# Later planned times for turned queries and keys, score banks and output transpositions in a hybrid attention step

## The chip, the cores and the metric

The kernel runs on one core of a Trainium2 chip. The metric is device time in microseconds (us). A core has five engines that each work through a queue of their own in the order in which the program issued it: TensorE (PE in the profile: matrix products), VectorE (DVE), ScalarE (ACT), GpSimd (POOL) and SyncE (SP), which here issues every DMA. They wait for each other through semaphores.

## The reference

The reference is one layer of a decoder step with 2048 prompt positions and 32 sample positions (8 sequences of 4). Two attention branches read the same normalised input; their outputs are gated, merged and projected:

```python
def prompt_layer(x, ...):
    qa, ka, va, ga, qb, kb, vb, gb, ma, mb = mixer_inputs(x, ...)   # rmsnorm, x @ w_in, QK-norm
    o_a, _ = banded_window_attention(qa, ka, va, 1, 128, rel_bias[:, :8], sink)
    for gi, (win, dil) in enumerate(((128, 1), (512, 4), (2048, 16))):
        o, lse = banded_window_attention(qb[:, :, gi, :, None, :], kb[:, :, gi], vb[:, :, gi],
                                         dil, win // dil, rel_bias[:, c0:c0 + 8], None)
    o_b = combine_dilations(outs, lses)        # weights proportional to softmax denominators
    y = mixer_output(x, o_a, o_b, ga, gb, ma, mb, w_up_a, w_up_b, w_out)

def mixer_output(x, o_a, o_b, ga, gb, ma, mb, w_up_a, w_up_b, w_out):
    ya = (o_a * silu(ga)) @ w_up_a
    yb = (o_b * silu(gb)) @ w_up_b
    return x + (sigmoid(ma) * ya + sigmoid(mb) * yb) @ w_out
```

Each query sees a window of 128 keys of its residue class, with a bias by distance. Branch A has 8 query heads of 64 on 2 key heads, branch B three groups of 8 heads. The 32 sample positions do the same against cached keys and values. Window rows of keys and values are outputs too.

## The kernel before, in words

**A planner writes the order.** The kernel is emitted by Python that carries a clock of its own. `Clock` (`ck`) has the planned time `ck.now`, a planned time at which ScalarE, VectorE and GpSimd become free (`use` adds a duration and gives the planned end) and a planned DMA queue (`move` sets `ck.come`, the planned landing of the transfer just issued). Generators are processes: what they yield is the planned time at which they go on. `ck.now` advances with every matmul that is issued (`mm`) and where the main thread waits for a condition. None of this exists on the chip. It decides only in which order instructions are put on each queue; the waits on the chip follow from the data. If the planner believes a result to be there earlier than it is, the instruction that reads it stands at the head of its queue and holds up what is behind it.

**Splits.** Products keep accuracy with two float16 parts of each operand, hi and lo (`split`, lines 303 to 308), and three matmuls for each product.

**Stages.** First the input is normalised and turned into `hT`, and the merge gates are computed (0 to some 400 us). Then come branch B's groups 3, 2 and 1, and branch A (to some 1840 us), each over 16 tiles of 128 positions. Last are the up-projections and the output projection. In the attention the main thread (`tile_order`, `steps`) issues projections tile by tile: query, key and value (in A also two gates), each 24 matmuls into a PSUM bank, on line 259 with the operands `slot` (weights) and `hT`. The work behind each is a chain that runs beside the main thread:

- `q_chain`: raw copy (L730), norm (L738 to L751), split by `parts`, then `turn` (line 764): one DMA transposition, SP's line 167, after which the chain waits until `ck.come`; then `qn`, the scratch of normed queries, is given back and `t.q` is set.
- `k_chain`: the same for keys, after `prev.scored` (all scores of the tile before issued); `k_turn` (line 769) calls `turn` and then issues two copies on VectorE (L773) that exchange the two halves of the partitions. Then `kn` is given back and `t.k` is set.
- `attend` starts when `t.q` and `t.k` are set and the tile before is scored. It spawns 2 units where a tile sees one key block, else 4.
- `unit`: takes one of two score banks (`S_l`), issues the score matmuls (L259, operands `arena`, shapes 128x128 or 128x256), then on VectorE the bias add with row maximum (L801), which empties the bank. `S_l[y].put()` gives it back in the plan. Then exponentials on ScalarE (L815), the split, a DMA transposition of the probabilities, a margin of 1800 ns, and the matmuls with the values (L259, shape 128x64) into bank 7.
- `to_pairs`, in branch A's `finish2` and once for the samples: VectorE scales the gated outputs (L1340), then, after a margin of 200 ns, eight transpositions on TensorE (L263) and splits into `hT`.

Beside all this run the sample positions' attention (GpSimd and VectorE, with reads of the caches) and the conversion of weights (L470, L473). At a change of group the bias tables are loaded anew, when the last tile has used them.

## Time and profile before

| | us |
|---|---|
| median of 3 runs (2163.1 to 2168.06) | 2163.2 |
| profiled execution | 2170.46 |
| its span, first to last instruction | 2168.6 |

The profile shows one execution. Busy time and idle time are in us; a wait is named by the line that waited and the line that ended its wait. "L259" is the helper that issues nearly all matmuls, so its groups are told apart by the names of tiles and by shapes: `bank<-slot,hT` are projections, `bank<-arena` is attention. `arena` is one large scratch tile that holds nearly all that moves between the engines.

### The profile page before, as it was taken

Reading aid. Unit: us, or ns where it says so; the run is one execution under the profiler, and the core shown is the slowest. Engines: PE = TensorE matmul, PEld = TensorE weight load, DVE = VectorE, ACT = ScalarE, POOL = GpSimd, SP = SyncE. Lnnn points to the kernel's source line nnn. Section 1 sums busy time; section 2 is a strip of 40 time slices with the busy share of each in tenths; the row PEclk is TensorE's granted clock in tenths of the full one; section 3 lists DMA queues with packets and bytes.
Section 4 is the critical chain, followed back from the end, with each engine's and each line's share of the span. In section 5 each row is a group of like instructions: output and inputs, shape, how many; then the busy total and the mean of one; then the engine's idle time right before and its main releaser. Section 6 shows DMA issues by size and latency. Waiting matters only on the chain.

```text
span 2168.6 us, 36145 instructions
## 1 busy us (share of the span) xinstructions
PE 2029.2 (94%) x13042; PEld 1135.8 (52%) x13042; DVE 1386.0 (64%) x3305; ACT 1053.3 (49%) x2526; POOL 707.9 (33%) x530
## 2 busy tenths in 40 slices
PE   6999999999999899898999999997899997999999
PEld 3555555666665455554544554544455555444464
DVE  5546662576754577773767885869788898642331
ACT  5432312555555667665776766765456555300000
POOL 1000000255632245541324552426655653220110
PEclk9999999999999999999999999999999998999999
DMA  7896571368879568978857878744434366332322
GB/s 225 175 300 230 203 269 57 115 175 201 217 174 264 139 134 203 215 157 228 218 113 151 168 167 160 172 102 107 79 82 108 96 176 175 110 107 88 115 85 93
DMA packets 528389, 344.34 MB, mean 159 GB/s; under 512 B 397585, under 2 KB 427762, under 8 KB 528210
## 3 DMA queue, kind: packets, MB, share of 16 engines
q1 hardware_dynamic: 528210, 342.04, 61.4%
q8 instruction: 102, 1.67, 0.3%
q14 instruction: 77, 0.63, 0.1%
HBM read 193.53 MB, written 62.43 MB: 118 GB/s over the span
## 4 chain that ended last, share of the span: by engine, by line
PE 59%; DVE 15%; DMA 12%; ACT 5%; issue 4%; SPq 2%; POOL 2%; DVEq 0%; POOLq 0%; ACTq 0%
PE bank L259 58%; DMA arena<-arena 7%; DVE arena L308 3%; DVE arena L773 2%; DMA out_dram<-arena 2%; DVE slot L473 2%; DVE arena L801 2%; ACT arena L815 2%; SPq L161 1%; SPq L167 1%; ACT slot L470 1%; DMA hT<-arena 1%; ACT arena L303 1%; DVE arena L751 1%; POOL nst L743 1%
## 5 line engine op out<-in xcount | busy, mean ns | idle before, releaser
L259 PE MATMUL bank<-slot,hT 128*128 128x512 f16 (+1 forms) x4992 | 1127.6, 377 | 8.0 <-ACT arena L730 4.5
L259 PEld LDWEIGHTS <-hT 128*128 128x128 f16 x4992 | 546.8, 113 | 436.5 <-issue 45.2
L259 PE MATMUL bank<-hT,slot 128*128 128x416 f16 (+4 forms) x2928 | 530.8, 342 | 17.7 <-DVE slot L473 3.8
L743 POOL TENSOR_TENSOR nst<-nst,nhalf 128x8 f32<-128x8 f32 (+2 forms) x136 | 232.4, 1710 | 773.9 <-DVE nst L741 704.6
L259 PEld LDWEIGHTS <-slot 128*128 128x128 f16 x2928 | 287.2, 99 | 251.1 <-DVE slot L473 11.1
L259 PEld LDWEIGHTS <-arena 128*128 128x128 f16 x4336 | 267.9, 99 | 283.1 <-issue 88.9
L259 PE MATMUL bank<-arena 128*128 128x64 f16 (+5 forms) x3746 | 269.9, 230 | 88.6 <-DVE arena L773 44.5
L815 ACT ACTIVATE arena<-arena,ast,inv 128x256 f32<-128x256 f32 (+1 forms) x512 | 283.8, 555 | 7.0
L308 DVE SCALAR_TENSOR_TENSOR arena<-arena 128x512 f16<-128x512 f32 (+1 forms) x292 | 221.6, 772 | 92.2 <-ACT arena L303 91.2
L303 ACT ACTIVATE arena<-arena 128x512 f16<-128x512 f32 (+2 forms) x395 | 231.3, 607 | 98.6 <-DMA arena<-arena 53.8
L1172 POOL TENSOR_TENSOR arena<-arena 128x512 f32<-128x512 f32 (+1 forms) x102 | 140.1, 1373 | 120.7 <-DVE arena L1215 101.4
L259 PE MATMUL bank<-slot,arena 128*128 128x512 f16 x768 | 167.9, 379 | 2.1 <-DVE slot L473 1.6
L473 DVE SCALAR_TENSOR_TENSOR slot<-slot,gsc 128x512 f16<-128x512 f32 (+1 forms) x144 | 107.3, 745 | 86.7 <-ACT slot L470 86.2
L730 ACT ACTIVATE arena<-bank 128x512 f32<-128x512 f32 x112 | 65.8, 589 | 173.4 <-PE bank L259 89.4
L643 ACT ACTIVATE arena<-bank,wst 128x416 f32<-128x416 f32 (+2 forms) x82 | 48.7, 597 | 190.5 <-PE bank L259 162.9
L470 ACT ACTIVATE slot<-slot,gsc 128x512 f16<-128x512 f32 (+1 forms) x144 | 98.1, 681 | 73.2 <-DVE slot L473 63.7
L303 ACT ACTIVATE arena<-arena,yk 128x512 f16<-128x512 f32 (+2 forms) x40 | 25.5, 638 | 201.1 <-POOL arena L1706 186.4
L1706 POOL TENSOR_TENSOR arena<-arena 128x512 f32<-128x512 f32 (+2 forms) x40 | 48.7, 1218 | 221.2 <-DVE arena L1692 201.7
L801 DVE CUSTOM_DVE_ANT_0 arena<-bank,bias 128x128 f32<-128x128 f32 (+1 forms) x296 | 87.4, 343 | 50.2 <-PE bank L259 48.9
L740 DVE TENSOR_REDUCE nst<-arena 128x8 f32<-128x512 f32 (+2 forms) x136 | 85.6, 630 | 42.3 <-ACT arena L738 41.6
L773 DVE COPY arena<-arena 64x1024 f16<-64x1024 f16 (+1 forms) x128 | 77.5, 605 | 54.0 <-DMA arena<-arena 52.3
L810 ACT ACTIVATE ast<-ast,ninv 128x2 f32<-128x2 f32 (+1 forms) x212 | 61.2, 289 | 102.6 <-DVE ast L801 101.7
(167 smaller groups left out, 1758.5 us busy)
## 6 DMA issues: line engine op xcount, KB each, us to landing
arena<-in_cache_b_kv_dram SPq DMA_DIRECT2D x144, 256.0 KB
slot<-in_w_in_dram SPq DMA_DIRECT2D x64, 512.0 KB
arena<-Qs SPq DMA_DIRECT2D x96, 256.0 KB
arena<-in_w_in_dram SPq DMA_DIRECT2D x16, 1024.0 KB
gates<-arena SPq DMA_DIRECT2D x78, 208.0 KB
comb<-arena SPq DMA_DIRECT2D x48, 264.0 KB
arena<-comb SPq DMA_DIRECT2D x48, 264.0 KB
arena<-gates SPq DMA_DIRECT2D x24, 512.0 KB
```

What stands on the lines that cost most here:

```text
L259: T.matmul(out, l, r, start=start, stop=stop)
L303: A.activation(hi, src, AF.Copy, scale=scale)
L308: V.scalar_tensor_tensor(lo, src, scale, hi, op0=OP.mult, op1=OP.subtract)
L470: A.activation(b.part(0, k), src, AF.Copy, scale=sc)
L473: V.scalar_tensor_tensor(b.part(1, k), src, sc, b.part(0, k), op0=OP.mult, op1=OP.subtract)
L730: A.activation(dst, src, AF.Copy)
L740: V.tensor_reduce(st[:, 0, :nh], heads(s), axis=AX.X, op=OP.add)
L743: G.tensor_tensor(st[:, 2, :nh], st[:, 1, :nh], nhalf[p0:p0 + n].to_broadcast([n, nh]), op=OP.pow)
L773: V.tensor_copy(y[64 - 64 * j:128 - 64 * j], x[64 * j:64 * j + 64])
L801: V.tensor_tensor_reduce(out=o, in0=i_, in1=b_, scale=1.0, scalar=-3e38 if g else sinkS[:, u, j:j + 1], op0=OP.add, op1=OP.max, accum_out= ...
L815: A.activation(e, e, AF.Exp, bias=nm[:, x:x + 1], scale=inv[:, g:g + 1], accum_out=l[:, x:x + 1])
L1172: G.tensor_tensor(sprod[:n], q, k, op=OP.mult)
```

## The change

Three planned times change. After a turned block the chain goes on 1500 ns later; a score bank counts as free 500 ns after the point at which it did; the margin ahead of the output transpositions is 900 ns for 200. No instruction is added, removed or altered.

```diff
     def turn(dst, src, nh):
 
         SP.turn(dst, src[:, :nh * 64].bitcast(F16))
-        yield ck.come
+        yield ck.come + 1500
...
         while t.biased in t.used:
             t.biased += 1
         yield e
-        S_l[y].put()
+        ck.at(ck.now + 500, S_l[y].put)
         A.activation(nm[:, xs_], m[:, xs_], AF.Copy, scale=ninv[:, g:g + 1])
...
         yield use("V", tv(512) + 500)
-        yield ck.now + 200
+        yield ck.now + 900
         for i in range(2):
             b = yield from tbank()
```

## The prediction

> **What bounds the kernel now.** I read the page first: the busy shares, the chain that ended last, then the span and mean granted clock of the core.

> ```profile
> span 2168.6 us, 36145 instructions
> PE 2029.2 (94%) x13042; PEld 1135.8 (52%) x13042; DVE 1386.0 (64%) x3305; ACT 1053.3 (49%) x2526; POOL 707.9 (33%) x530
> PE 59%; DVE 15%; DMA 12%; ACT 5%; issue 4%; SPq 2%; POOL 2%; DVEq 0%; POOLq 0%; ACTq 0%
> core 0: 2168.6 us, clock 0.979
> ```

> TensorE (PE) is busy for 2029.2 of 2168.6 us. So 139 us are idle, and that is nearly all that a change of order can win. The chain agrees: 59% PE, most of the rest links that PE stood waiting for. Next I read the waits of PE and of VectorE (DVE): who waited, for what, us in total, how often, the longest.

> ```profile
> PE bank L259 <- DVE arena L773: 44.5, 32, 4.7
> PE bank L259 <- DMA arena<-arena: 27.8, 20, 6.5
> PE bank L259 <- DVE ast L801: 12.6, 7, 4.0
> PE bank L263 <- DVE arena L1340: 7.4, 6, 2.4
> DVE arena L773 <- DMA arena<-arena: 52.3, 34, 4.6
> ```

> The largest wait is for L773, the copies that swap the halves of a turned key block; DVE in its turn stands 52.3 us waiting for the turning DMA ahead of them. L801 is the bias add that empties a score bank; L1340 scales the pairs that to_pairs transposes. These three belong to the three edits. The DMA row is mixed, so I took PE's groups with shapes kept apart:

> ```profile
> L259 PE MATMUL bank<-arena 128*128 128x64 f16 x2544 | 112.5, 196 | 24.1 <-DMA arena<-arena 23.7 <-DVE arena L1459 0.2
> L259 PE MATMUL bank<-arena 128*128 128x256 f16 x672 | 106.8, 277 | 36.4 <-DVE arena L773 22.2 <-DVE ast L801 12.6 <-DMA arena<-arena 1.0
> L259 PE MATMUL bank<-arena 128*128 128x128 f16 x352 | 30.2, 226 | 25.6 <-DVE arena L773 22.3 <-DMA arena<-arena 3.2
> ```

> Shapes 128x128 and 128x256 are scores, 128x64 is probabilities times values. So 4.2 us (1.0 + 3.2) of the DMA waits are scores waiting for the turned block itself, and 23.7 us are value products waiting for turned probabilities, whose margin (1800 ns in unit) the change leaves alone. Now one ordinary tile in the timeline, 18.3 us from the first of its score rows to that of the next tile (start, duration, instruction, count, idle before it and its releaser):

> ```profile
> 554.67 0.55 PE L259 MATMUL bank<-arena 128*128 128x128 f16 x7 [0.94 <-DVE arena L773]
> 559.34 0.61 PE L259 MATMUL bank<-arena 128*128 128x128 f16 x8
> 559.79 9.88 PE L259 MATMUL bank<-slot,hT 128*128 128x512 f16 x45
> 570.81 2.13 DVE L773 COPY arena<-arena 64x1024 f16<-64x1024 f16 x2 [1.70 <-DMA arena<-arena]
> 571.84 0.22 PE L259 MATMUL bank<-arena 128*128 128x128 f16 x1
> 572.99 0.55 PE L259 MATMUL bank<-arena 128*128 128x128 f16 x7 [0.94 <-DVE arena L773]
> 574.68 0.51 PE L259 MATMUL bank<-arena 128*128 128x64 f16 x12
> ```

> DVE had nothing to do for 1.70 us, then copied from 570.81 to 572.94. PE had reached the scores at 571.84, ran the one matmul that needs no copy, and stood 0.94 us. Projection matmuls for the coming tile were there (45 of them in 9.88 us, 0.22 us each), but they stand behind the scores in PE's queue. The kernel's planner believed the turn and the copies to be done earlier than they were.

> **The change part by part.** No instruction is added or removed, and no new wait on the chip; only the planner's clock moves, and with it the order on each queue. Line 773 has 128 copies, two for each of 64 tiles, so turn is delayed 128 times in the plan, once for queries and once for keys of each tile.

> *Turned queries and keys, +1500 ns.* Nearly seven projection matmuls (1.5/0.22) now go ahead of each tile's scores. On DVE the copies fall behind what is ready in 1.5 us; where DVE idled, as at 570.81, they run at the same moment as before. The transposing DMA itself does not move; the probabilities' DMAs, bias reloads and stores behind the scores move on SP's queue with their tile. A wait of up to 1.5 us goes, a longer one loses 1.5. Ten of the 32 L773 waits are longer:

> ```profile
> 496.69 0.55 PE L259 MATMUL bank<-arena 128*128 128x128 f16 x7 [1.64 <-DVE arena L773]
> 516.54 0.72 PE L259 MATMUL bank<-arena 128*128 128x128 f16 x7 [1.79 <-DVE arena L773]
> 689.47 0.91 PE L259 MATMUL bank<-arena 128*128 128x128 f16 x7 [4.72 <-DVE arena L773]
> 740.83 0.55 PE L259 MATMUL bank<-arena 128*128 128x128 f16 x7 [3.36 <-DVE arena L773]
> 811.75 0.49 PE L259 MATMUL bank<-arena 128*128 128x256 f16 x3 [1.95 <-DVE arena L773]
> 911.09 0.91 PE L259 MATMUL bank<-arena 128*128 128x128 f16 x7 [3.79 <-DVE arena L773]
> 1113.23 0.49 PE L259 MATMUL bank<-arena 128*128 128x256 f16 x3 [1.99 <-DVE arena L773]
> 1469.62 1.44 PE L259 MATMUL bank<-arena 128*128 128x256 f16 x15 [2.71 <-DVE arena L773]
> 1502.15 1.39 PE L259 MATMUL bank<-arena 128*128 128x256 f16 x11 [4.15 <-DVE arena L773]
> 1568.59 1.44 PE L259 MATMUL bank<-arena 128*128 128x256 f16 x15 [3.04 <-DVE arena L773]
> ```

> They sum to 29.1; the other 22 to 15.4. Saved: 10 x 1.5 + 15.4 = 30.4 us. The 4.2 us for the turned block fall under the same margin, but some stand right before a copy wait of the same scores and would be counted twice:

> ```profile
> 473.45 0.22 PE L259 MATMUL bank<-arena 128*128 128x128 f16 x1 [0.97 <-DMA arena<-arena]
> 475.00 0.55 PE L259 MATMUL bank<-arena 128*128 128x128 f16 x7 [1.33 <-DVE arena L773]
> ```

> Here 0.97 + 1.33 is cut by 1.5, not by 2.3. I take 2.2 off for all such pairs: **30.4 + 4.2 - 2.2 = 32.4 us**. Cover gone (no projections left to put ahead), the saving there is 0.

> *Score banks free 500 ns later.* The shortest of the 7 L801 waits exceeds 0.5:

> ```profile
> 1082.46 0.60 PE L259 MATMUL bank<-arena 128*128 128x256 f16 x4 [0.57 <-DVE ast L801]
> ```

> So **7 x 0.5 = 3.5 us**, with projections as cover again.

> *Output transpositions 700 ns later* (900 for 200; 17 passes through to_pairs). Two of the six L1340 waits are shorter than that:

> ```profile
> 1587.30 0.63 PE L263 MATMUL bank<-ident,arena 128*128 128x128 f32 x4 [0.25 <-DVE arena L1340]
> 1745.37 0.63 PE L263 MATMUL bank<-ident,arena 128*128 128x128 f32 x4 [0.32 <-DVE arena L1340]
> ```

> The others save 0.7 at most: **4 x 0.7 + 0.57 = 3.4 us**.

> *The clock.* Stretches around long waits (length, busy times, granted clock, DMA share):

> ```profile
> 516.00:521.00 5.00, 4.46 (x29) 2.67 (x29) 4.14 (x16) 2.41 (x4) 1.23 (x1) 0.66 0.54 184
> 686.00:696.00 10.00, 6.53 (x31) 3.72 (x31) 6.86 (x25) 5.53 (x15) 5.06 (x3) 0.66 0.88 261
> 908.00:918.00 10.00, 6.91 (x37) 3.42 (x37) 6.22 (x16) 5.03 (x16) 6.60 (x5) 0.66 0.78 180
> 1502.00:1508.00 6.00, 5.85 (x38) 3.63 (x38) 5.76 (x18) 2.67 (x7) 3.32 (x4) 0.72 0.05 14
> ```

> Each costs (1 - clock) x length: 1.7, 3.4, 3.4, 1.7, together 10.2 us, of which I take **6**, since waits of 2.3 to 3.2 us remain at the last three (bounds 0 and 10.2). [...]

> *What is given back.* First, at the changes of stage, when few projections are ready, a later chain is a later end. Four stretches, 680:760, 960:1010, 1460:1575 and 1789:1843, have together (sum row of the windows):

> ```profile
> sum 299.00, PE 242.19 PEld 142.62 DVE 213.77 ACT 162.85 POOL 124.47; mean PE 60.55 PEld 35.65 DVE 53.44 ACT 40.71 POOL 31.12
> ```

> 57 us of PE idle, the densest in the attention. I charge one turn and one bank margin for each: 4 x (1.5 + 0.5) = **8 us** (bounds 0 and 50, below). Second, the value product at 574.68 belongs to the scores at 559.34, and the wait at 572.99 lies between them. Take it away, and PE reaches the product 0.94 us earlier against the same chain of DVE, ScalarE and DMA. The 23.7 us of waits for turned probabilities can grow; I take **5 us** (bounds 0 and 12: 13 such waits of the 20 DMA waits, 0.94 each).

> Sum: 32.4 + 3.5 + 3.4 + 6 - 8 - 5 = 32.3 us off the span of 2168.6, that is 2136.3. The profiled execution took 2170.5 us as a whole, so 2138; against the median of the runs, 2163.2, it is **2131**.

> **The rivals.** *Everything behind the copies comes loose.* DVE stands 52.3 us in front of them with ready work behind, so ScalarE and the probability chains also run ahead, and the waits go whole: 44.5 + 4.2 - 2.2 + 12.6 + 7.4 + 10.2 = 77 us, nothing given back: 2086. For it: the idle row of L773. Against: the longest waits exceed the margins by up to 3 us. Between this and the forecast lies about 2105.

> *The waits only change their name.* In the ordinary stretch the DMA engines are nearly full:

> ```profile
> 552.00:592.00 40.00, 37.19 (x242) 25.47 (x241) 29.43 (x71) 23.03 (x61) 25.66 (x18) 1.00 0.85 221
> ```

> If transfers at 0.85 set the pace, a faster PE finds turned probabilities that much later, the 23.7 us grow by what was won, and the time is 2160 to 2166. Against: the stretch still has 15% free, and the tile would need only 5% more (0.94 of 18.3 us).

> *Slower: the chain of tiles at a change of stage decides.* Key turns wait for the tile before to be scored. If the last three and first two tiles run one after another there, each pays the turn and two bank margins, 1.5 + 2 x 0.5 = 2.5 us: 5 x 2.5 = 12.5 for a change, 50 for four. The gains inside these stretches go too: the waits at 689, 740, 1469, 1502 and 1568 (5 x 1.5), a few tenths beside, and the 6 us of clock. Left elsewhere: 32.4 - 8.3 + 3.5 + 3.4 - 5 = 26. Net 24 slower: 2187. It decides against the change from (26 + 6.5)/4 = 8 us for each change. Against it: in the ordinary tile the last scores end at 559.95 and the copies of the next start at 570.81, so 10.9 us lie between, against a turn of a few us; PE's work, not that chain, sets the period of 18.3.

> **How the numbers follow.** A measurement of this kernel can tell 0.3%, 6.5 us, from no change. The forecast (2112 to 2148) has 0.55, the larger gain 0.13 (2080 to 2112), a gain of 2148 to 2156 0.07, changed names 0.13 (within 0.3%), slower 0.12. So faster 0.75, same 0.13, slower 0.12. The range 2100 to 2168 leaves out the slower case and the far end of the larger gain; cost bounds of 50 and 12 against 45 of gains reach past its upper end only in the slower case.

> **What would show it.** The L773 row of PE's waits falls from 44.5 to about 14, DVE's wait in front of the copies from 52.3 by a third or more; L801 to about 9; L1340 to about 4; scores waiting for a turned block to near 0; 128x64 products waiting for DMA rise to about 29; the mean granted clock rises from 0.979 to about 0.982. Wrong: if the L773 row falls and PE's idle total stays at 139, the names only changed; if idle time in the four stretches exceeds 57 + 32, the slower case holds; if waits of several us remain at ordinary tiles, the order shifted elsewhere.

## The result: 1.4% slower

The changed kernel takes 2195.24 us (median of 4 runs, 2192.91 to 2196.6), the kernel before 2163.41 in the same rounds. The ratio is **1.0141** (95% interval 1.0123 to 1.0158). The forecast was 2131, with slower at a chance of 0.12 and the range ending at 2168. Here is the changed kernel's page and its core row:

```profile
span 2194.0 us, 36053 instructions
PE 2027.6 (92%) x13042; PEld 1134.7 (52%) x13042; DVE 1388.6 (63%) x3305; ACT 1051.9 (48%) x2526; POOL 713.1 (33%) x530
core 0: 2194.0 us, clock 0.974
```

The busy time of every engine is that of before to within 1%. The span grew by 25.4 us, and all of it is TensorE standing idle. Its waits, and VectorE's in front of the key copies:

```profile
PE bank L259 <- DVE arena L773: 37.9, 23, 5.0
PE bank L259 <- DMA arena<-arena: 36.8, 23, 5.1
PE bank L259 <- ACT arena L999: 15.4, 4, 6.0
PE bank L259 <- ACT arena L730: 10.5, 8, 6.6
PE bank L263 <- DVE arena L1340: 7.1, 4, 2.8
PE bank L259 <- DVE ast L801: 3.6, 2, 2.7
DVE arena L773 <- DMA arena<-arena: 25.2, 15, 4.4
```

VectorE's idle time in front of the copies halved (52.3 to 25.2), and the waits behind a score bank fell from 12.6 to 3.6. But the wait for the copies fell only from 44.5 to 37.9 where about 14 was forecast, and two rows grew: projections that wait for L999 and L730. These are ScalarE's raw copies out of a PSUM bank, L999 of a value block, L730 of a query or key block, and a projection waits for them when no bank is free. In the kernel before the two rows had 6.7 us together, now they have 25.9. ScalarE's own waits tell why. First TensorE's two rows and ScalarE's two in the kernel before:

```profile
PE bank L259 <- ACT arena L730: 4.5, 1, 4.5
PE bank L259 <- ACT arena L999: 2.2, 1, 2.2
ACT arena L730 <- DMA out_dram<-arena: 80.1, 13, 10.6
ACT arena L999 <- DMA out_dram<-arena: 24.0, 7, 10.3
```

then ScalarE's in the changed one:

```profile
ACT arena L730 <- DMA out_dram<-arena: 93.2, 14, 9.5
ACT arena L999 <- DMA out_dram<-arena: 56.4, 15, 9.7
```

The raw copies write into staging rows, `stK` for keys and `stV` for values, one each, from which window rows are stored to memory. The next copy into a row must wait until the store of the tile before has landed. The planner gives a row back (`stK_l.put()`, `stV_l.put()`) where it issues the store, not where the store lands. So the copy gets to the head of ScalarE's queue too early and holds up all that is behind it. In group 3 every one of the 16 tiles stores both rows, in group 2 four, in group 1 one.

Where in time was it lost? Each group has one sample projection (L891) at its third tile, so from one of them to the next is one group's work. The first two in the kernel before (start, duration):

```profile
420.12 2.12 PE L891 MATMUL bank<-slot,hT 128*32 128x512 f16 x27
766.73 5.36 PE L891 MATMUL bank<-slot,hT 128*32 128x512 f16 x72
```

and in the changed one:

```profile
418.26 0.83 PE L891 MATMUL bank<-slot,hT 128*32 128x512 f16 x9
788.33 5.36 PE L891 MATMUL bank<-slot,hT 128*32 128x512 f16 x72
```

Group 3 took 370.1 us for 346.6. Worked out in the same way, groups 2 and 1 together took 686.8 for 684.0, and from there to the first output projection 434.0 for 433.0. **23.5 of the 25.4 us were lost in group 3.** Counted in projection matmuls, 72 to a tile, its first eight tiles took 4.8 us less than before. Tiles 9 to 14 took 139.8 us for 116.2, with TensorE's waits in them 24.2 for 5.0. From there to the third tile of group 2, with the end of the group and the change to the next, it was 94.7 for 91.2. So the loss came ahead of the change of group. The timeline of an ordinary tile there, in the changed kernel (start, duration, instruction, idle before it and its releaser):

```profile
564.82 0.47 SPq L161 DMA_DIRECT2D out_dram<-arena  x1
568.12 0.69 ACT L999 ACTIVATE arena<-bank,wst 128x512 f32<-128x512 f32 x1 [4.23 <-DMA out_dram<-arena]
569.37 0.69 DVE L308 SCALAR_TENSOR_TENSOR arena<-arena 128x512 f16<-128x512 f32 x1 [3.01 <-ACT arena L303]
578.83 0.22 PE L259 MATMUL bank<-arena 128*128 128x128 f16 x1 [0.82 <-DMA arena<-arena]
579.14 0.42 SPq L161 DMA_DIRECT2D out_dram<-arena  x1
581.30 0.55 PE L259 MATMUL bank<-arena 128*128 128x128 f16 x7 [2.25 <-DVE arena L773]
583.37 0.60 ACT L730 ACTIVATE arena<-bank 128x512 f32<-128x512 f32 x1 [5.58 <-DMA out_dram<-arena]
```

The value rows' store goes out at 564.82; the next value copy has stood on ScalarE for 4.23 us until it ran at 568.12. The softmax parts (L303) and the split on VectorE behind it (L308) come late by it. The key row's store goes out at 579.14, and the next key copy costs ScalarE 5.58 us more. TensorE has issued 60 projection matmuls since the last scores, where the tile of before that the prediction shows had 45, and still finds the turned block (0.82) and the copies (2.25) missing. In that tile of before it lost 0.94.

### The profile page after: what moved, and what is told of

The parts are those of the page before. It is cut to its first block, busy times and chain, and to the rows that moved or that the text cites. A ratio compares the mean times of both kernels' runs of the same rounds, so it can differ in the third digit from the quotient of the medians.

```text
span 2194.0 us, 36053 instructions
## 1 busy us (share of the span) xinstructions
PE 2027.6 (92%) x13042; PEld 1134.7 (52%) x13042; DVE 1388.6 (63%) x3305; ACT 1051.9 (48%) x2526; POOL 713.1 (33%) x530
## 4 chain that ended last, share of the span: by engine, by line
PE 52%; DVE 15%; DMA 12%; ACT 7%; issue 6%; POOL 5%; SPq 3%; ACTq 0%; POOLq 0%; DVEq 0%
PE bank L259 50%; DMA arena<-arena 4%; DMA out_dram<-arena 4%; DVE arena L308 3%; ACT arena L815 2%; DVE arena L801 2%; ACT arena L303 2%; POOL nst L743 2%; SPq L167 2%; SPq L161 1%; DVE slot L473 1%; POOL arena L1172 1%; DVE arena L773 1%; DVE arena L751 1%; DMA hT<-arena 1%
## 5 line engine op out<-in xcount | busy, mean ns | idle before, releaser
L259 PE MATMUL bank<-slot,hT 128*128 128x512 f16 (+1 forms) x4992 | 1128.8, 377 | 30.3 <-ACT arena L999 15.4
L259 PEld LDWEIGHTS <-hT 128*128 128x128 f16 x4992 | 547.6, 113 | 468.1 <-issue 74.9
L259 PE MATMUL bank<-hT,slot 128*128 128x416 f16 (+4 forms) x2928 | 529.0, 341 | 26.7 <-DVE slot L473 10.7
L743 POOL TENSOR_TENSOR nst<-nst,nhalf 128x8 f32<-128x8 f32 (+2 forms) x136 | 232.4, 1709 | 762.9 <-DVE nst L741 694.8
L259 PEld LDWEIGHTS <-slot 128*128 128x128 f16 x2928 | 287.0, 99 | 259.1 <-issue 16.1
L259 PEld LDWEIGHTS <-arena 128*128 128x128 f16 x4336 | 266.7, 100 | 268.1 <-issue 64.4
L259 PE MATMUL bank<-arena 128*128 128x64 f16 (+5 forms) x3746 | 265.6, 233 | 80.0 <-DVE arena L773 37.9
L308 DVE SCALAR_TENSOR_TENSOR arena<-arena 128x512 f16<-128x512 f32 (+1 forms) x292 | 227.6, 791 | 158.1 <-ACT arena L303 149.0
L303 ACT ACTIVATE arena<-arena 128x512 f16<-128x512 f32 (+2 forms) x395 | 232.4, 607 | 85.0 <-DVE arena L751 36.1
L259 PE MATMUL bank<-slot,arena 128*128 128x512 f16 x768 | 167.9, 379 | 2.2 <-DVE slot L473 1.6
L730 ACT ACTIVATE arena<-bank 128x512 f32<-128x512 f32 x112 | 65.6, 588 | 148.5 <-DMA out_dram<-arena 93.2
L303 ACT ACTIVATE arena<-arena,yk 128x512 f16<-128x512 f32 (+2 forms) x40 | 25.5, 637 | 199.7 <-POOL arena L1706 185.0
L801 DVE CUSTOM_DVE_ANT_0 arena<-bank,bias 128x128 f32<-128x128 f32 (+1 forms) x296 | 87.3, 342 | 39.0 <-PE bank L259 38.6
L1750 DVE SCALAR_TENSOR_TENSOR slot<-bank,sst,slot 128x512 f32<-128x512 f32 (+1 forms) x33 | 24.8, 750 | 125.7 <-PE bank L259 115.9
L306 DVE TENSOR_TENSOR arena<-arena 128x512 f16<-128x512 f32 (+1 forms) x103 | 82.0, 799 | 30.7 <-ACT arena L303 27.0
```

The lines of the kernel that those rows point to most:

```text
L259: T.matmul(out, l, r, start=start, stop=stop)
L303: A.activation(hi, src, AF.Copy, scale=scale)
L306: V.tensor_tensor(lo, src, hi, op=OP.subtract)
L308: V.scalar_tensor_tensor(lo, src, scale, hi, op0=OP.mult, op1=OP.subtract)
L730: A.activation(dst, src, AF.Copy)
L743: G.tensor_tensor(st[:, 2, :nh], st[:, 1, :nh], nhalf[p0:p0 + n].to_broadcast([n, nh]), op=OP.pow)
```

## The experiments

Theory L, with which I began: the one staging row of keys is a loop (raw copy, norm, store, landing, next raw copy) that the margin of `turn` stretches in group 3. Rival C: the changes of stage, as in the prediction's slower case. Rival O: any new order of the queues costs about as much. "B" is the stretch from the first sample projection to branch A's, three groups of work, in the profiled execution (1030.6 us before, 1056.9 with the change); "A" is from there to the first output projection (433.0 and 434.0). Ratios are to the kernel before on the same chip in the same rounds; times in us that belong to a ratio are that ratio of 2163. B and A come from one execution of each kernel, and 19 executions of the kernel before on one chip ranged from 2165.0 to 2179.6 us, so a difference of a few us in B or A is not sure.

### One edit at a time

Each keeps one of the three changed lines:

```diff
-        yield ck.come
+        yield ck.come + 1500                      # e1_turn
-        S_l[y].put()
+        ck.at(ck.now + 500, S_l[y].put)           # e2_bank
-        yield ck.now + 200
+        yield ck.now + 900                        # e3_pairs
```

> Only the 1500 ns behind turned queries and keys. Theory L (the loop through the one staging row of keys in group 3: raw copy, norm, gain on GpSimd, store, landing, next raw copy; 17.9 us a tile before, 21 to 23 us after) expects nearly the whole loss here: 2185 to 2195 us, and the raw copies of keys (L730) in group 3 some 21 us apart. Rival C (the changes of stage, where every margin lies on the chain) expects about half, 2175. Rival O (any new order of the queues costs about as much) expects something like 2180 for each of the three edits alone.

> Only the 500 ns behind a score bank. Theory L: the loop is hardly touched, 2157 to 2166 us, L801 waits of TensorE shrink from 12.6. Rival C: about 2170. Rival O: about 2180.

> Only the 700 ns more ahead of the output transpositions. Theory L: nothing before branch A changes, 2159 to 2165 us. Rival C: about 2166. Rival O: up to 2180 although only branch A's order can move.

| | ratio (95%) | B | A |
|---|---|---|---|
| e1_turn | 1.0081 (1.0060 to 1.0102) | 1053.4 | 429.5 |
| e2_bank | 0.9989 (0.9972 to 1.0007) | 1027.8 | 431.0 |
| e3_pairs | 1.0044 (1.0026 to 1.0062) | 1028.8 | 446.4 |

The margin behind turned blocks alone makes branch B as slow as the whole change does. The bank margin does nothing that can be measured. The output margin costs 0.44%, all of it in branch A. Its own wait shrank there, L1340 from 7.4 to 1.7 us, while others grew: turned probabilities in the same stretch from 9.5 to 15.3. So e2 went as theory L expected, e1 in the place but less in size (2181 us for 2185 to 2195), and e3 against it (2173 for 2159 to 2165). Rival O's 2180 fits e1 and not e2 (2161). Rival C's 2175 for e1 and 2170 for e2 are both missed.

### The margin everywhere but in group 3

```diff
-            yield from turn(t.QT, qn, 8)
+            yield from turn(t.QT, qn, 8, 0 if g == 3 else 1500)
...
-            yield from k_turn(8, t.KT, cur)
+            yield from k_turn(8, t.KT, cur, 0 if g == 3 else 1500)
```

> All of the change, but no margin behind turned blocks in group 3 (it stays in groups 2, 1 and branch A). Theory L: the loss of some 27 us in group 3 is gone, 2155 to 2170 us. Rival C: one change of stage of four is spared, about 2187. Rival O: about 2190.

Measured: 1.0088 (1.0065 to 1.0110), outside what L expected. By the stretches, group 3 is cured (342.6 us, before 346.6, changed 370.1), but group 2 took 355.0 for 346.9 and group 1 344.5 for 337.1, so B is 1042.1. Of two claims only one held: group 3's loss comes from its own turned blocks; but sparing it doesn't save the kernel. The time is 2182 us (2178 to 2187), so rival C's "about 2187" is not excluded here. Counted in projection matmuls, e4 keeps level with the kernel before to the end of group 3. It is 10.6 us ahead after ten tiles of group 2, 9.9 behind after fifteen, and loses 8 more in the first two tiles of branch A. Both places hold row stores as well as a change of stage, so e4 alone does not tell the two apart. For group 2 the later runs e9 and e15 do, in the kernel with all margins: with the values' rows alone eased, it takes 336.7 and 336.2 us, against 351.8 in the changed kernel.

### A second staging row

Once a weight block is converted, the last 512 words of its slot are free. Every second tile uses such a strip as its row, so that no copy has to wait for the tile before (the edit of e5 and e6; ... stands for lines left out):

```diff
+        two = g == 3 and len(made) % 2 == 0
+        sK_l = stK2_l if two else stK_l
+        def k_buf():
+            return slots[blocks[f"k{g}"].slot][:].bitcast(F32)[:, 4096:4608] if two else stK
...
-            yield from norm(b.ap[:, :], 0, P, 8, blocks[f"k{g}"], kn, stK, raw=(b.lock, kn_l))
+            yield from norm(b.ap[:, :], 0, P, 8, blocks[f"k{g}"], kn, sK, raw=(b.lock, kn_l))
```

e7 and e8 do the same for values, in all three groups. In e5 to e8 the strip is also used at tile 14, after the slot was given to the next block, so the last raw rows of that block's weights are overwritten: values of later outputs change, the instructions do not. e9, e11, e12 and e16 leave tile 14 out.

> The kernel before with a second staging row for the keys of every other tile of group 3 (a free strip of the weight slot), so that a raw copy no longer waits for the store of the tile before. Theory L (that loop sets the tile's period in group 3: 17.9 to 19.8 us against some 17.2 us of TensorE work): 15 to 25 us faster than before, the L730 waits for stores in group 3 nearly gone. Rival C (only the plan's order counts, the loop is a by-product): within 6 us of before.

> The changed kernel with the same second row. Theory L: the loss in group 3 (some 20 us) is gone, so about 2160 to 2175 us on the scale of before 2163; what is lost later, at the end of group 2, stays. Rival C: as the changed kernel, 2190 to 2195.

> The changed kernel with a second row for keys and for values, in groups 3, 2 and 1. Theory L extended to values (the wait of the value copy, L999, for a store of up to 9.7 us at the row tiles of group 2): group 2's loss goes too, 2145 to 2165 us, and the margins then gain what was forecast. Rival C: as the changed kernel.

> The kernel before with both second rows. Theory L: 2135 to 2150 us; with e7 it shows what the margins do once the rows are no loop: if the forecast's reasons hold, e7 is faster than e8 by up to 30 us. Rival C: within 6 us of before.

> The changed kernel with a second staging row for values alone (tiles 0, 2 to 12 of each group of branch B). In group 3 the gains of the stored keys on GpSimd stood 18.8 us apart before, 21.4 with the change, 20.8 with a second row for keys, 18.5 with both. Theory V (the value row is what the margin stretches: it is given back only after the values of the tile before are used, which the margin puts off, and the next value copy then stands on ScalarE until the store has landed): 18.3 to 19.2 us apart and 2150 to 2168 us on the scale of 2163 before. Theory K+V (both rows are needed): over 20 us apart and 2175 to 2185.

> The changed kernel with both second rows, at tiles 0, 2 to 12 alone, so that no strip is used after its weight slot has been given away. Theory V: as e7, 2138 to 2150 us on the scale of 2163 before, a little more at the ends of the groups. If e7's time came from the overwritten weights' order: up to 2165.

> As e11, without the 700 ns more ahead of the output transpositions. They alone cost 0.44% (0.26 to 0.62). If that cost adds up: 2130 to 2142 us, some 9 below e11. If it belongs to the order of the queues in that one kernel: within 4 us of e11.

| | margins | second rows | ratio (95%) | B |
|---|---|---|---|---|
| e5_before_2k | none | keys, group 3 | 0.9926 (0.9896 to 0.9955) | 1014.4 |
| e8_before_2kv | none | both | 0.9908 (0.9883 to 0.9933) | 1011.0 |
| e6_after_2k | all | keys, group 3 | 1.0071 (1.0048 to 1.0094) | 1040.4 |
| e9_after_2v | all | values | 0.9938 (0.9916 to 0.9960) | 1013.9 |
| e7_after_2kv | all | both | 0.9885 (0.9855 to 0.9914) | 1002.8 |
| e11_after_2kv_to12 | all | both | 0.9886 (0.9854 to 0.9918) | 997.0 |
| e12_turn_bank_2kv | no output margin | both | 0.9832 (0.9811 to 0.9854) | 994.4 |

Without the margins the second row of keys is worth 0.74%, with them it takes back only half of the loss. So L, with keys alone, falls short. The row of values takes back all of it and 0.6% more (e9), and both together 2.6% (1.0141 to 0.9885). With both, the change is no longer slower but a little faster (0.9885 against 0.9908, intervals that overlap; 8 us in B). e7, at 2139, is faster than its 2145 to 2165; e5 and e8 lie within what L expected. e11 and e7 agree, so the overwritten weights did not make the time. e9's time, 2150, was at the lower end of theory V's interval. Its interval for the gains on GpSimd failed: they stood 20.0 us apart where 18.3 to 19.2 was expected. The key copies still stood 102 us for stores on ScalarE, which may be why.

### The landing in the plan

The rows stay single, but the planner gives them back later:

```diff
             SP.dma_start(rows[:, :512], stK)
+            yield ck.come + 1000
             stK_l.put()
...
                 SP.dma_start(rows[:, 512:], stV)
-            stV_l.put()
             t.v = True
+            if rows is not None:
+                yield ck.come + 1000
+            stV_l.put()
```

> The changed kernel with one row each, but in the plan a row counts as free only 1 us after its store is planned to land, so that the next raw copy is put on ScalarE's queue later and holds up less behind it. If the blocked queue of ScalarE is the cost (waits of L730 and L999 for stores, 93 and 56 us in the changed kernel): 2165 to 2178 us. If the time for which the row is taken is the cost, whoever waits for it: 2190 to 2200.

> The kernel before, with a row counted as free only 1 us after its store is planned to land; no margin of the change. Theory M (the margins gain some 20 us where the rows do not stop ScalarE): this alone gains at most 10 us, 2153 to 2163 on the scale of 2163 before, and the changed kernel with it (0.9916) is the faster one. Theory N (the margins gain nothing, all of 0.9916 is the row's own gain): 2140 to 2150 us.

> The changed kernel with the landing in the plan for the row of values alone. Theory V (the value copy is what newly stops ScalarE: L999's waits for stores went from 24 to 56 us): most of the recovery, 2155 to 2170 us. If the keys' copies (L730, 80 and 93 us) weigh as much: 2175 to 2185.

> The changed kernel with the row's landing in the plan, and without the 700 ns more ahead of the output transpositions. With second rows, leaving them out was worth 0.54%. If that holds here: 2130 to 2140 us on the scale of 2163 before; if it belonged to that one order: 2142 to 2150.

> Both second rows, the landing in the plan, the margins of turns and banks. The rows hardly wait for stores any more (L730 19 us, L999 6 us in e12), so little is left to gain: 2128 to 2136 us on the scale of 2163 before.

| | margins | ratio (95%) | B | A |
|---|---|---|---|---|
| e13_before_landed | none | 1.0046 (1.0024 to 1.0067) | 1025.7 | 448.6 |
| e10_after_landed | all | 0.9916 (0.9898 to 0.9934) | 1010.0 | 434.5 |
| e15_after_landed_v | all, landing of values alone | 1.0038 (1.0019 to 1.0056) | 1031.2 | 434.4 |
| e14_turn_bank_landed | no output margin | 0.9897 (0.9868 to 0.9926) | 1012.0 | 435.6 |
| e16_turn_bank_2kv_landed | no output margin, second rows | 0.9823 (0.9796 to 0.9849) | 985.4 | 444.9 |

This is the plainest test. The rows are as many as before and no instruction differs; the edit moves the raw copies to a later place on ScalarE's queue, and what follows from them in the plan moves with them. ScalarE's and TensorE's waits of e10:

```profile
ACT arena L730 <- DMA out_dram<-arena: 25.4, 10, 5.1
ACT arena L1000 <- DMA out_dram<-arena: 4.9, 2, 4.6
PE bank L259 <- DVE arena L773: 16.1, 14, 2.8
PE bank L259 <- DMA arena<-arena: 23.0, 17, 6.1
```

ScalarE's waits for stores fell from 149.6 us (93.2 + 56.4) to 30.3, and then the wait for the copies came down to 16.1, near the 14 that was forecast. The loss of 1.41% is a gain of 0.84%. So what the change lost is lost to the **blocked queue of ScalarE**, more than to the time for which a row is taken. The time is 2145 us, better than either expectation. e15, at 2172 between its two, shows that both copies count: the landing of values alone takes back 1.0 of the 2.25 points.

e13 answers whether the cure alone made the gain: without the margins it gains 4.9 us in B, and as a whole it is 0.46% slower, for its branch A took 448.6. Its total lies outside both expectations, so by their own terms neither theory M nor theory N held. A reading by B alone, chosen after the result, favours M: in B the margins cost 26.3 us with the rows as they were (1030.6 to 1056.9) and gain 15.7 where the plan knows the landing (1025.7 to 1010.0). e13 shows two limits as well. ScalarE's waits for stores fell in it as far as in e10, from 104.1 to 31.7 us, but B gained only 4.9, where second rows gain 19.6 without margins (e8): in the kernel before, putting the copies later in the queue was worth little by itself. And the wait for the copies fell to 21.9 with no margin at all, so of the fall to 16.1 in e10 the margins made the smaller part.

Leaving the output margin out (e14) is worth 0.2% in this order, less than its uncertainty, against 0.5% with second rows (e11 to e12); its 2141 lies between its two expectations. The kernels e12 and e16, at 2127 and 2125 us a little below what was expected of them, beat both kernels of the case, by 1.7 and 1.8% against before.

## Why the prediction was wrong, step by step

```profile
L259 PE MATMUL bank<-arena 128*128 128x64 f16 x2544 | 112.4, 196 | 34.1 <-DMA arena<-arena 34.0
```

- **The rivals.** The slower case gave 2187 and the time was 2195, but that is chance, as its mechanism was the wrong one: it put the loss at the changes of stage and called the ordinary tile safe. The loss lies in tiles 9 to 14 of group 3, ahead of the change. The last of the prediction's signs of being wrong is the one that came: waits of several us at ordinary tiles, as the 2.25 above. "The 10.9 us between the last scores and the next copies" spoke of the loop through the key block alone; the rows were another.

What stays open: why e4 loses more in groups 2 and 1, where only five of 32 tiles store rows, than the changed kernel does there, and what decides branch A's time.

## What to carry to other kernels

A margin in a written-out order moves more than the instruction that it is meant for: follow each buffer that the delayed chain gives back, to the engine that fills it next, and look what that engine holds up while it waits. Read the waits of engines that are far from busy too; a half idle ScalarE that stands 150 us in front of stores can hold up the whole kernel although its busy share is 48%. Such a row says where to look and not what it costs: e10 and e13 both took it down to some 30 us, and against the kernel that it started from the first gained 46.9 us in B, the second 4.9. A planner should give a buffer back when the last reader is done, and where that reader is a store, that is its landing.

## What the runs showed of the hardware

The time from a store's issue to the copy that it released was longer than I had thought: 564.82 to 568.12 and 579.14 to 583.37 in the changed kernel's timeline, 3.3 and 4.2 us for 256 KB. A planner should add the measured time to the planned end of a store whose buffer is used again.

In the changed kernel's trace the pair of key copies took nearly twice the time or more (1.59 to 2.35 us for 0.86) beside most of GpSimd's wide instructions, and not beside its narrow ones. Two places of the timeline, VectorE and then GpSimd:

```profile
558.47 0.86 DVE L773 COPY arena<-arena 64x1024 f16<-64x1024 f16 x2
...
579.43 1.82 DVE L773 COPY arena<-arena 64x1024 f16<-64x1024 f16 x2
```

```profile
556.63 1.26 POOL L1172 TENSOR_TENSOR arena<-arena 128x512 f32<-128x512 f32 x1
560.12 1.66 POOL L1172 TENSOR_TENSOR arena<-arena 128x512 f32<-128x512 f32 x1 [2.23 <-DVE arena L1215]
...
579.48 1.49 POOL L1172 TENSOR_TENSOR arena<-arena 128x512 f32<-128x512 f32 x1 [1.23 <-DVE arena L1215]
```

At 558.47 GpSimd has a pause (a row ends at 557.89, the next begins at 560.12), and the two copies take 0.86 us. At 579.43 one of its products starts at the same time, and they take 1.82. Over the 48 pairs of branch B in the changed kernel, the 19 with no GpSimd instruction beside them took 0.85 to 0.86 us. So did the 21 that ran beside only a power of eight columns (L743, 1.63 to 2.09 us on GpSimd). Of the other eight, beside an instruction of 512 columns, six took 1.59 to 2.35. Why, and why the other two took 0.86, no run shows. The planner gives the pair 0.66 us in either case, which may be one more reason why the copies come late for it.
